# A decoder block in one kernel: the decays' scan in one piece, TensorE's order written out in the SSD scan

## The chip, the cores and the metric

The kernel runs on one core of a Trainium2 chip. The metric is the time of one execution on the device, in microseconds (us); the median of three runs is compared. TensorE (PE in the profile) multiplies matrices and accumulates in PSUM banks of 128x512; VectorE (DVE), ScalarE (ACT) and GpSimd (POOL) work element by element on tiles of 128 partitions in SBUF; SyncE (SP) issues the DMA transfers between DRAM and SBUF. Each engine works through its own list of instructions in order and waits on semaphores for the others.

## The reference, cut to what matters

The reference is one block of a hybrid model for 1024 tokens of width 1024: a Mamba-2 branch (SSD) and a gated linear attention branch (GLA), merged by gates, then attention to a memory, and a feed-forward part. The change touches the two recurrences:

```python
proj = n @ w_in
z, xBC, dt_raw, q, k, v, r, a1, g_ssd, g_gla = jnp.split(proj, idx, axis=-1)

# SSD, in chunks
xBC = silu(causal_dwconv(xBC, conv_w, conv_b))
a_cs = jnp.cumsum(dt * A, axis=-1)
CB = einsum('bclgn,bcsgn->bcgls', Cc, Bc)
y_diag = einsum('bcgls,bgrcls,bcsgrp->bclgrp', CB, segsum_exp(a), X)
states = einsum('bclgn,bgrcl,bclgrp->bcgrpn', Bc, decay_states, X)
prev = scan over chunks: state * chunk_decay + states
y_off = einsum('bclgn,bcgrpn,bgrcl->bclgrp', Cc, prev, exp(a_cs))
y = rmsnorm((y_diag + y_off + D * x) * silu(z), norm_g)

# GLA, the decays
log_alpha = log_sigmoid(a1 @ w_a2 + b_a) / 16
bcum = jnp.cumsum(log_alpha in chunks, axis=2)
```

All is float32. The kernel uses chunks of 128 tokens.

## The kernel before

**Products.** `proj` is computed in units of 256 output columns. A unit (class `Unit`) is a 2x2 block product done with seven products instead of eight; for a unit by itself they come in the order B11, T2, T1, B21, T3, B22, T4. A product is 12 matmuls of 128x512: four slices of the contraction, times three, since each float32 operand is split into a high and a low part (`h`, `l`) and the low-low part is left out. ScalarE makes the high part of the weights (`whi`), VectorE the low one (`wlo`), both after a 1 MB load `raw`; sums of weights (`sa`, and `raw` in place) are made by GpSimd or VectorE. ScalarE (B11, B21) and VectorE (the other five, `o<-acc,o`) take the results out of PSUM.

**Side work among the products.** `run(main, (side, rate))` takes `main` product by product and lets a generator `side` go on by `rate` of its yields after each. The stages that matter, by first unit: four units `zu` with the preparation of both recurrences as side work (`ssd_prep`, `gla_prep`); six units `xu`, each with the convolution of the unit ahead (`conv`: on VectorE, three passes for each of two blocks); then `ru` (4), `qk` (4) and `gs[:1]` with the SSD steps; `gs[1:]` and `gg[:3]` with the GLA steps; `gg[3]`; then the dense stages, whose first operands are `hl` and `wd`.

**SSD.** Each of the 16 steps (8 chunks by 2 groups of heads) has `load`, `lay` (transposes into banks; `cbm`, `bt`, `xd`), `decay` (eight ScalarE passes per step that make `e`, two exponentials, two VectorE products), `scan` (16 + 16 + 4 small matmuls into two banks, and the state), `gate` (`y`, on VectorE, then GpSimd), `stat` (a matmul with `ones`, then `rs` on VectorE and GpSimd) and `norm` (a matmul that spreads `rs`, `y<-y,bank`, store). In its turn, step i scans, the step before has its statistics, the next one is laid, step i is gated, the step before is normed, and the next one's decay is made, with yields between.

**Order.** A scheduler of the framework orders each engine's list from priorities; side work has a higher priority (`prio=PRIO`), and so have weights' splits and evacuations (`ahead()`, by 200). `pinned` keeps an instruction at its place in the program's order. The loads are all issued by SP's queue.

## Time and profile before

| | |
|---|---|
| three runs, median | 1956.74 us (1956.26 to 1957.37) |
| the profiled execution, its own time | 1956.3 us |
| its span in the trace | 1954.5 us |
| granted TensorE clock, mean | 0.996 |
| busy TensorE, VectorE, ScalarE, GpSimd | 98%, 67%, 43%, 29% |

In the trace the unit `xu[0]` begins at 249.6 us, `ru[0]` at 365.9, `ru[1]` at 385.4, `gs[0]` at 591.0, `gs[2]` at 634.1 and `gg[3]` at 789.3. An engine's share of busy time is an average over stages with different limits. The chain of waits follows the work that ended last backwards from the end; a row "acc<-T3h,wlo" is a matmul into bank `acc` with stationary operand T3 (high part) and moving operand `wlo`, or the other way round, as the names are given in the trace; a number in brackets at a row's end is the idle time ahead of it and what ended it.

### The profile page before, as it was taken

The page shows a single profiled execution, that of the slowest core. Times are in us where ns is not written, and L with a number is a line of the kernel's source. Part 1 is how long each engine was busy: PE and PEld are TensorE (multiplying, and loading weights), DVE is VectorE, ACT ScalarE, POOL GpSimd, SP SyncE. Part 2 cuts the span into 40 slices and gives each one's busy share as a digit, 9 for nine tenths or more (in the row PEclk, how much of TensorE's full clock was granted, in tenths as well). Part 3 has the DMA queues.
Part 4 walks back from the last instruction along what each step waited for, and adds up shares of the span by engine and source line. Part 5 has one row for each costly group of instructions (what it writes and reads, how often), then busy time and mean ns, then how long its engine had stood idle before and what let it go on. Part 6 is the DMA issues. An engine that isn't in the chain of part 4 may idle for free.

```text
span 1954.5 us, 26271 instructions
## 1 busy us (share of the span) xinstructions
PE 1919.9 (98%) x9772; PEld 1617.3 (83%) x9772; DVE 1317.2 (67%) x1868; ACT 848.4 (43%) x1493; POOL 574.1 (29%) x429
## 2 busy tenths in 40 slices
PE   8899999999999999999999999999999999999998
PEld 7898788778788888888888888888888888888887
DVE  6866779879886655565545237577777777766565
ACT  8434564465552543643224226454333333344243
POOL 1012334355553212112433000006445544320002
PEclk9999999999999999999999999999999999999999
DMA  9333372366553653897684201442233224177463
GB/s 316 139 121 101 119 290 98 133 196 198 169 168 114 209 162 119 328 371 252 242 298 150 78 24 44 140 141 81 87 125 112 82 100 143 42 270 243 159 222 119
DMA packets 238242, 317.97 MB, mean 163 GB/s; under 512 B 16906, under 2 KB 156404, under 8 KB 238116
## 3 DMA queue, kind: packets, MB, share of 16 engines
q1 hardware_dynamic: 238116, 316.31, 47.8%
q8 instruction: 77, 1.26, 0.3%
q14 instruction: 49, 0.40, 0.1%
HBM read 215.27 MB, written 100.99 MB: 162 GB/s over the span
## 4 chain that ended last, share of the span: by engine, by line
PE 83%; DVE 8%; DMA 3%; issue 2%; ACT 2%; POOL 2%; SPq 1%; POOLq 0%; DVEq 0%; ACTq 0%
PE acc L51 72%; PE bank L51 9%; DVE wlo L73 2%; DVE cv L73 1%; PE bank L55 1%; DVE o L73 1%; DMA xt<-in_x_dram 1%; DMA csb<-cs_d 1%; DVE hs L73 1%; DMA raw<-in_w_in_dram 1%; POOL sa L73 0%; ACT e L911 0%; POOL y L73 0%; POOL ssum L73 0%; DVE y L73 0%
## 5 line engine op out<-in xcount | busy, mean ns | idle before, releaser
L51 PE MATMUL acc<-hl,wd 128*128 128x512 f32 x1920 | 438.7, 390 | 0.0
L51 PEld LDWEIGHTS acc<-hl,wd 128*128 128x128 f32 x1920 | 360.4, 188 | 74.1
L73 DVE TENSOR_TENSOR wlo<-raw,whi 128x512 fp32r<-128x512 f32 x272 | 241.6, 894 | 80.7 <-ACT whi L221 78.7
L221 ACT ACTIVATE whi<-raw 128x512 fp32r<-128x512 f32 x272 | 169.5, 628 | 245.1 <-PE acc L51 214.3
L73 DVE TENSOR_TENSOR o<-acc,o 128x512 f32<-128x512 f32 (+1 forms) x256 | 172.8, 676 | 119.8 <-PE acc L51 108.2
L51 PE MATMUL acc<-fs 128*128 128x512 f32 (+1 forms) x792 | 155.7, 356 | 0.1
L51 PEld LDWEIGHTS acc<-fs 128*128 128x128 f32 x792 | 130.8, 189 | 20.7 <-issue 0.5
L73 POOL TENSOR_TENSOR raw<-raw,sa 128x512 f32<-128x512 f32 x44 | 58.7, 1334 | 228.6 <-DVE wlo L73 228.6
L73 DVE TENSOR_TENSOR fs<-fr,fs 128x1024 fp32r<-128x1024 f32 (+1 forms) x84 | 99.0, 1219 | 36.6 <-ACT fs L221 36.5
L221 ACT ACTIVATE fs<-fr 128x1024 fp32r<-128x1024 f32 (+1 forms) x84 | 78.8, 982 | 96.3 <-PE acc L51 32.1
L221 ACT ACTIVATE whi<-sa 128x512 fp32r<-128x512 f32 x96 | 60.0, 626 | 108.3 <-PE acc L51 102.7
L73 POOL TENSOR_TENSOR sa<-raw 128x512 f32<-128x512 f32 x43 | 67.8, 1577 | 105.0 <-DMA raw<-in_w_in_dram 78.0
L73 DVE TENSOR_TENSOR wlo<-sa,whi 128x512 fp32r<-128x512 f32 x96 | 82.2, 857 | 15.2 <-ACT whi L221 15.1
L73 DVE TENSOR_TENSOR wd<-raw,wd 128x1024 fp32r<-128x1024 f32 x40 | 53.1, 1329 | 50.9 <-ACT wd L221 50.8
L73 POOL TENSOR_TENSOR rstd<-rstd,mhalf 128x4 f32<-128x4 f32 (+1 forms) x7 | 8.7, 1246 | 251.2 <-DVE rstd L73 251.2
L221 ACT ACTIVATE wd<-raw 128x1024 fp32r<-128x1024 f32 x40 | 42.3, 1059 | 88.5 <-PE acc L51 82.7
L51 PE MATMUL acc<-B22h,wlo 128*128 128x512 f32 x192 | 76.6, 399 | 3.0 <-DVE wlo L73 3.0
L51 PE MATMUL acc<-T3h,wlo 128*128 128x512 f32 x192 | 76.0, 396 | 1.2 <-DVE wlo L73 1.2
L73 POOL TENSOR_TENSOR raw<-raw 128x512 f32<-128x512 f32 x44 | 75.9, 1725 | 2.8 <-DVE sa L73 2.8
L51 PE MATMUL acc<-T4h,whi 128*128 128x512 f32 x192 | 76.1, 396 | 0.4 <-DVE o L73 0.4
L51 PE MATMUL acc<-B22h,whi 128*128 128x512 f32 x192 | 76.1, 396 | 0.0
L51 PE MATMUL acc<-B11h,whi 128*128 128x512 f32 x192 | 75.8, 395 | 0.0
(389 smaller groups left out, 4735.4 us busy)
## 6 DMA issues: line engine op xcount, KB each, us to landing
raw<-in_w_in_dram SPq DMA_DIRECT2D x26, 1024.0 KB, 5.7
raw<-in_w_ffn_in_dram SPq DMA_DIRECT2D x22, 1024.0 KB, 8.1
act_d<-o SPq DMA_DIRECT2D x77, 256.0 KB, 2.2
fr<-act_d SPq DMA_DIRECT2D x35, 512.0 KB, 5.8
pre<-in_w_ffn_out_dram SPq DMA_DIRECT2D x11, 1024.0 KB
fr<-down_d SPq DMA_DIRECT2D x20, 512.0 KB, 4.7
down_d<-pre SPq DMA_DIRECT2D x33, 256.0 KB, 3.6
raw<-in_w_xkv_dram SPq DMA_DIRECT2D x8, 1024.0 KB, 8.1
```

The costliest lines, as they stand in the source:

```text
L51: return s.e.matmul(o, x, y, **kw)
L55: return s.e.transpose(o, x, i)
L73: return f(*a, **kw)
L221: ACT.activation(hi, src, AF.Copy)
```

## The change

- **The decays.** In `gla_prep` a head's cumulative sum is one scan over 1024 tokens instead of two over 512. The preparation so has four yields fewer, and its rate is 1.0 instead of 33/28.
- **Convolutions.** The units of B and C (4 and 5) come first. The pool with the states and the tiles `xz` and `bc` is opened ahead of the convolutions; the first step's loads are put behind the third and the fifth unit, its `csb` in an `xz` buffer. `bc` has three buffers and one DMA instead of two.
- **SSD steps.** Loads are issued two steps ahead; `csb` has a call of its own, behind the scan that frees its buffer. `cbm` stays in a part of its PSUM bank. Scan, the sum for the step before (`sum`) and the norm of the step two before stand together, then the next step's lay and this one's gate, then the statistics, the next decay and the state's update, then the square. There are six yields ahead of the first scan, and three instead of one in the first step.
- **Order.** During the SSD stage TensorE's list is in the program's order (`manual_schedule`).
- **Units.** The SSD steps have `gs[:2]` instead of `gs[:1]`, at a rate of 79/70 instead of 64/63; the GLA steps run over `gs[2:]` and `gg[:3]`, at 40/30 instead of 40/36.

```diff
--- before.py
+++ after.py
@@ -824,9 +824,8 @@
             yield
             pinned(DVE.scalar_tensor_tensor(x, x, 0.0, y, ALU.min, ALU.subtract))
             yield
-            for j in range(2):
-                pinned(DVE.tensor_tensor_scan(y[:, half(j)], keep[:, half(j)], x[:, half(j)], 0.0, ALU.mult, ALU.add))
-                yield
+            pinned(DVE.tensor_tensor_scan(y, keep, x, 0.0, ALU.mult, ALU.add))
+            yield
             yv, xv = (v.rearrange("p (c s) -> p c s", s=CH) for v in (y, x))
             bm, bl = yv[:, :, CH // 2 - 1:CH // 2], yv[:, :, CH - 1:CH]
             pinned(sub(DVE, xv, yv, bm.to_broadcast([P, NCH, CH])))
@@ -839,31 +838,22 @@
             ACT.activation(e, e, AF.Exp, scale=1.0 / TAU)
         yield
 
-    xu = [Unit(w_in, 0, XBC0 + 256 * u) for u in range(6)]
+    XU = (4, 5, 0, 1, 2, 3)
+    xu = [Unit(w_in, 0, XBC0 + 256 * u) for u in XU]
     zu = w_in_units(Z0, 4, store_rows(sz_d))
     ru = w_in_units(R0, 4, store_rows(sr_d))
     qk = w_in_units(Q0, 2, store_rows(q_d)) + w_in_units(K0, 2, store_rows(k_d))
     gs = w_in_units(GS0, 4, store_rows(gs_d))
     gg = w_in_units(GG0, 4, store_rows(gg_d))
     prep = chain([ssd_prep(), gla_prep()])
-    run(singles(zu, B, xu[:1]), (prep, 33 / 28))
+    run(singles(zu, B, xu[:1]), (prep, 1.0))
     drain(prep)
     settle_all()
     st2.close()
     st2 = ExitStack()
-    cvp = pool("conv", 1, stack=st2)
-    pend = iter(())
-    for u in range(6):
-        run(group([xu[u]], B, (xu + ru)[u + 1:u + 2]), (pend, 1.0))
-        drain(pend)
-        pend = conv(u, xu[u])
-    drain(pend)
-    st2.close()
-
-
     st3 = ExitStack()
-    sp_ = pool("ssd", 1, stack=st3)
-    state = [sp_.tile([P, GH, 64], F32, name=f"state{g}", tag=f"state{g}") for g in range(2)]
+    sl_ = pool("ssdl", 1, stack=st3)
+    state = [sl_.tile([P, GH, 64], F32, name=f"state{g}", tag=f"state{g}") for g in range(2)]
     for g in range(2):
         POOL.memset(state[g], 0.0)
 
@@ -880,23 +870,24 @@
 
         def load(s):
             g, tk = s.g, s.tk
-            s.L = sp_.tile([P, 8, CH], F32, name="xz", tag="xz", bufs=3)
+            s.L = sl_.tile([P, 8, CH], F32, name="xz", tag="xz", bufs=3)
             SP.dma_start(s.L[:, 0:4], xbc_d[g * 512:(g + 1) * 512, tk].rearrange("(k p) s -> p k s", p=P))
-            s.BC = sp_.tile([P, 2, CH], F32, name="bc", tag="bc", bufs=2)
-            for i in range(2):
-                r0 = 1024 + i * 256 + g * P
-                SP.dma_start(s.BC[:, i], xbc_d[r0:r0 + P, tk])
+            s.BC = sl_.tile([P, 2, CH], F32, name="bc", tag="bc", bufs=3)
+            SP.dma_start(s.BC, xbc_d[1024:1536, tk].rearrange("(i g p) s -> g p i s", g=2, p=P)[g])
+            SP.dma_start(s.L[:, 4:8], sz_d[g * 512:(g + 1) * 512, tk].rearrange("(k p) s -> p k s", p=P))
+
+        def load_cs(s):
             s.csb = sp_.tile([P, GH, CH], F32, name="csb", tag="csb", bufs=2)
+            s.fetch_cs()
+
+        def fetch_cs(s):
             SP.dma_start(s.csb.rearrange("p h s -> p (h s)"),
                          cs_d[s.i0:s.i0 + GH, :].rearrange("h s -> (h s)").partition_broadcast(P))
-            SP.dma_start(s.L[:, 4:8], sz_d[g * 512:(g + 1) * 512, tk].rearrange("(k p) s -> p k s", p=P))
 
         def lay(s):
-            p = bank()
+            p = s.p = bank()
             PE.matmul(p[:, :P], s.BC[:, 0], s.BC[:, 1], start=True, stop=True)
             PE.transpose(p[:, P:2 * P], s.BC[:, 0], ident)
-            s.cbm = sp_.tile([P, CH], F32, name="cbm", tag="cbm", bufs=2)
-            mul(DVE, s.cbm, p[:, :P], triu)
             s.bt = sp_.tile([P, P], F32, name="bt", tag="bt", bufs=2)
             ACT.activation(s.bt, p[:, P:2 * P], AF.Copy)
             p = bank()
@@ -914,7 +905,9 @@
             s.xc = sp_.tile([P, GH, 64], F32, name="xc", tag="xc", bufs=1)
             mul(POOL, s.xc, s.xd, s.heads(dec, 64))
             mul(DVE, s.csb, s.csb, s.BC[:, 1].unsqueeze(1).to_broadcast([P, GH, CH]))
-            mul(DVE, s.e, s.e, s.cbm.unsqueeze(1).to_broadcast([P, GH, CH]))
+            cbm = s.p[:, 2 * P:3 * P]
+            mul(DVE, cbm, s.p[:, :P], triu)
+            mul(DVE, s.e, s.e, cbm.unsqueeze(1).to_broadcast([P, GH, CH]))
 
         def scan(s):
             st = state[s.g]
@@ -930,7 +923,11 @@
                 PE.matmul(p[:, a * 256:(a + 1) * 256], s.bt, s.xc[:, 4 * a:4 * a + 4].rearrange("p h d -> p (h d)"),
                           start=True, stop=True)
             mul(POOL, st, st, s.heads(ec, 64))
-            add(DVE, st, p.rearrange("p (h d) -> p h d", d=64), st)
+            s.pst = p
+
+        def update(s):
+            st = state[s.g]
+            pinned(add(DVE, st, s.pst.rearrange("p (h d) -> p h d", d=64), st))
 
         def gate(s):
             s.y = sp_.tile([P, 4, CH], F32, name="y", tag="y", bufs=3)
@@ -938,10 +935,15 @@
                 DVE.scalar_tensor_tensor(s.y[:, k], s.L[:, k], dcol[:, s.g * 4 + k:s.g * 4 + k + 1],
                                          s.py[:, k * P:(k + 1) * P], ALU.mult, ALU.add)
             mul(POOL, s.y, s.y, s.L[:, 4:8])
-            sq = sp_.tile([P, 4, CH], F32, name="sq", tag="sq", bufs=1)
-            ACT.activation(sq, s.y, AF.Square)
+
+        def square(s):
+            s.sq = sp_.tile([P, 4, CH], F32, name="sq", tag="sq", bufs=1)
+            pinned(ACT.activation(s.sq, s.y, AF.Square))
+
+        def sum(s):
+            sq = s.sq
             s.rd = sp_.tile([P, CH], F32, name="rd", tag="rd", bufs=2)
-            add(DVE, sq[:, 0:2], sq[:, 0:2], sq[:, 2:4])
+            pinned(add(DVE, sq[:, 0:2], sq[:, 0:2], sq[:, 2:4]))
             add(DVE, s.rd, sq[:, 0], sq[:, 1])
 
         def stat(s):
@@ -957,38 +959,64 @@
             SP.dma_start(ys_d[s.g * 512:(s.g + 1) * 512, s.tk].rearrange("(k p) s -> p k s", p=P), s.y)
 
     def ssd_steps():
-        it = [SSD(c, g) for c in range(NCH) for g in range(2)]
-        it[0].load()
-        yield
+        n = len(it)
+        it[1].load()
+        it[1].load_cs()
+        for _ in range(1):
+            yield
         it[0].lay()
         yield
         it[0].decay()
-        yield
-        for i in range(len(it) + 1):
-            z = it[i - 1] if i else None
-            a = it[i] if i < len(it) else None
-            b = it[i + 1] if i + 1 < len(it) else None
-            if b:
-                b.load()
+        for _ in range(6):
+            yield
+        for i in range(n + 2):
+            y, z, a, b, c = (it[k] if 0 <= k < n else None for k in range(i - 2, i + 3))
             if a:
                 a.scan()
+            if z:
+                z.sum()
+            if y:
+                y.norm()
+            yield
+            if c:
+                c.load()
+            if b:
+                b.lay()
+            if a:
+                a.gate()
             yield
             if z:
                 z.stat()
             if b:
-                b.lay()
-            yield
+                b.decay()
+            if c:
+                c.load_cs()
             if a:
-                a.gate()
-            yield
-            if z:
-                z.norm()
-            if b:
-                b.decay()
-            yield
-
+                a.update()
+            for _ in range(3 if i == 0 else 1):
+                yield
+            if a:
+                a.square()
+                yield
+
+    it = [SSD(c, g) for c in range(NCH) for g in range(2)]
+    cvp = pool("conv", 1, stack=st2)
+    pend = iter(())
+    for n, u in enumerate(XU):
+        run(group([xu[n]], B, (xu + ru)[n + 1:n + 2]), (pend, 1.0))
+        drain(pend)
+        pend = conv(u, xu[n])
+        if n == 2:
+            it[0].csb = sl_.tile([P, GH, CH], F32, name="xz", tag="xz", bufs=3)
+            it[0].fetch_cs()
+        if n == 4:
+            it[0].load()
+    drain(pend)
+    st2.close()
+    sp_ = pool("ssd", 1, stack=st3)
     ssd = ssd_steps()
-    run(singles(ru + qk + gs[:1], B, gs[1:2]), (ssd, 16 * 4 / 63), prio=PRIO)
+    with tc.manual_schedule(engines={mybir.EngineType.PE}):
+        run(singles(ru + qk + gs[:2], B, gs[2:3]), (ssd, 79 / 70), prio=PRIO)
     drain(ssd)
     st3.close()
 
@@ -1113,7 +1141,7 @@
             yield
 
     gla = gla_steps()
-    run(singles(gs[1:] + gg[:3], B, gg[3:]), (gla, 8 * 5 / 36), prio=PRIO)
+    run(singles(gs[2:] + gg[:3], B, gg[3:]), (gla, 8 * 5 / 30), prio=PRIO)
     drain(gla)
     st4.close()
     st_early.close()
```

First place: VectorE in the preparation, in the last but one of the `zu` units, before (names: `gx`, `gy` are the decays of a head, a scan stands as SCALAR_TENSOR_TENSOR from `keep`, `wlo` are the low parts of weights, `o` the unit's output; of the unit `raw_2333` here, the low parts are those of B21, T3 and B22).

```order
L73 SCALAR_TENSOR_TENSOR gy0_2101<-keep_2058,gx0_2097 128x512 x2
L73 TENSOR_TENSOR gx0_2097<-gy0_2101 128x1024
L73 TENSOR_TENSOR wlo_2405<-raw_2333,whi_2404 128x512
L73 TENSOR_TENSOR o_2341<-acc_2369,o_2341 128x512
L73 SCALAR_TENSOR_TENSOR gx1_2098<-gx1_2098,gy1_2102 128x1024
L73 TENSOR_TENSOR wlo_2429<-raw_2333,whi_2428 128x512
L73 TENSOR_TENSOR o_2341<-acc_2388,o_2341 128x512
L73 SCALAR_TENSOR_TENSOR gy1_2102<-keep_2058,gx1_2098 128x512 x2
L73 TENSOR_TENSOR wlo_2449<-raw_2333,whi_2448 128x512
```

And with the change (the same unit is `raw_2331`, the low parts are those of B21, T3, B22 and T4):

```order
L73 SCALAR_TENSOR_TENSOR gy0_2101<-keep_2058,gx0_2097 128x1024
L73 TENSOR_TENSOR gx0_2097<-gy0_2101 128x1024
L73 TENSOR_TENSOR wlo_2402<-raw_2331,whi_2401 128x512
L73 TENSOR_TENSOR o_2335<-acc_2367,o_2335 128x512
L73 TENSOR_TENSOR wlo_2422<-raw_2331,whi_2421 128x512
L73 TENSOR_TENSOR o_2335<-acc_2386,o_2335 128x512
L73 SCALAR_TENSOR_TENSOR gx1_2098<-gx1_2098,gy1_2102 128x1024
L73 TENSOR_TENSOR wlo_2446<-raw_2331,whi_2445 128x512
L73 SCALAR_TENSOR_TENSOR gy1_2102<-keep_2058,gx1_2098 128x1024
L73 TENSOR_TENSOR wlo_2465<-raw_2331,whi_2464 128x512
```

T3's low part has moved from behind head 1's `gx` to ahead of it, and B22's from behind head 1's scan to ahead of it; the scan is one row.

Second place: TensorE in the SSD stage, before, where a step's `xz` transposes (lay) and the spread of `rs` (norm) stand (`bank` are PSUM banks of the SSD step, `acc` those of the units).

```order
L51 MATMUL acc_4103<-T4h_1355,wlo_4301 128x512
L51 MATMUL acc_4103<-T4h_1355,whi_4300 128x512
L51 MATMUL acc_4103<-T4l_1356,whi_4300 128x512
L55 MATMUL bank_4177<-ident_107,xz_4117 128x128 [waits DMAHW5_49,DVE_49,PE_49]
L55 MATMUL bank_4177<-ident_107,xz_4117 128x128 x3
L51 MATMUL acc_4103<-T4h_1355,wlo_4301 128x512
L51 MATMUL acc_4344<-B11h_436,whi_4340 128x512 [waits Activation_49]
L51 MATMUL acc_4344<-B11l_437,whi_4340 128x512
L51 MATMUL acc_4344<-B11h_436,wlo_4341 128x512
L51 MATMUL bank_4232<-ident_107,rs_4167 128x128 [waits Pool_49]
```

With the change, in unit `q0`, the end of a scan and what follows it:

```order
L51 MATMUL bank_4647<-csb_4449,state0_2642 64x128 x2
L51 MATMUL bank_4664<-xc_4601,bt_4548 128x256 [waits Activation_49,Pool_49]
L51 MATMUL bank_4664<-xc_4601,bt_4548 128x256
L51 MATMUL bank_4671<-ident_107,rs_4587 128x128 [waits Pool_49]
L51 MATMUL bank_4680<-bc_4542 128x128 [waits DMAHW6_49,DVE_49]
L55 MATMUL bank_4680<-ident_107,bc_4542 128x128
L55 MATMUL bank_4685<-ident_107,xz_4540 128x128 [waits DMAHW1_49,DVE_49,PE_49]
L55 MATMUL bank_4685<-ident_107,xz_4540 128x128 x3
L51 MATMUL acc_4571<-T3h_1258,whi_4699 128x512 [waits Activation_49]
L51 MATMUL acc_4571<-T3l_1259,whi_4699 128x512
```

Before, matmuls of products stood between lay and norm; now scan, norm and the next lay follow one another here, and the next product comes behind them.

Third place: VectorE at the end of `gg[3]` and the begin of the first dense stage, before (`hl` and `wd` are its operands, `acc_7544` and `acc_7518` banks of the unit).

```order
L73 TENSOR_TENSOR o_7481<-acc_7544,o_7481 128x512 [waits PE_49]
L73 TENSOR_TENSOR wlo_7616<-raw_7469,whi_7615 128x512 [waits Activation_49]
L73 TENSOR_TENSOR wd_7611<-raw_7500,wd_7611 128x1024 [waits DMAHW2_49,Activation_49]
L73 TENSOR_TENSOR wd_7664<-raw_7500,wd_7664 128x1024 [waits DMAHW6_49,Activation_49]
L73 TENSOR_TENSOR wlo_7634<-raw_7469,whi_7633 128x512 [waits PE_49,Activation_49]
L73 TENSOR_TENSOR o_7481<-acc_7518,o_7481 128x512 [waits DVE_49,PE_49]
L73 SCALAR_TENSOR_TENSOR hl_7506<-hl_7506,cols_118 128x1024 [waits DMAHW3_49,Activation_49]
L73 TENSOR_TENSOR o_7481<-acc_7544,o_7481 128x512 [waits PE_49]
L73 SCALAR_TENSOR_TENSOR hl_7532<-hl_7532,cols_118 128x1024 [waits DMAHW6_49,Activation_49]
```

And with the change (`o_7452` with `acc_7489` in its last row here is the evacuation of T4):

```order
L73 TENSOR_TENSOR o_7452<-acc_7515,o_7452 128x512 [waits PE_49]
L73 SCALAR_TENSOR_TENSOR hl_7529<-hl_7529,cols_118 128x1024 [waits DMAHW1_49,Activation_49]
L73 TENSOR_TENSOR o_7452<-acc_7489,o_7452 128x512 [waits PE_49]
L73 SCALAR_TENSOR_TENSOR hl_7533<-hl_7533,cols_118 128x1024 [waits DMAHW2_49,Activation_49]
L73 TENSOR_TENSOR wd_7582<-raw_7471,wd_7582 128x1024 [waits DMAHW4_49,Activation_49]
L73 TENSOR_TENSOR wd_7635<-raw_7471,wd_7635 128x1024 [waits DMAHW3_49,Activation_49]
```

The first low parts of `wd` stood ahead of the unit's last low part; now they stand behind its last evacuation and one more `hl`.

## The prediction

> **What bounds the kernel now.** I read the page first: the busy table (engine, busy us, share, count) and the chain of work that ended last.
>
> ```profile
> span 1954.5 us, 26271 instructions
> PE 1919.9 (98%) x9772; PEld 1617.3 (83%) x9772; DVE 1317.2 (67%) x1868; ACT 848.4 (43%) x1493; POOL 574.1 (29%) x429
> PE 83%; DVE 8%; DMA 3%; issue 2%; ACT 2%; POOL 2%; SPq 1%; POOLq 0%; DVEq 0%; ACTq 0%
> ```
>
> TensorE is the bound: whatever helps must shorten TensorE's own work or its waits. The change touches no product, so its matmul work stays. All that is to be won or lost are the times in which TensorE stands, in the stages that the change touches. So next I read the view by windows, cut at the stages (columns: window, length, busy us of PE, PEld, DVE, ACT, POOL, then granted clock, DMA share, GB/s).
>
> ```profile
> 208.00:227.00 19.00, 15.90 (x68) 12.26 (x67) 16.37 (x15) 10.19 (x14) 10.19 (x9) 1.00 0.35 119
> 229.00:231.00 2.00, 2.00 (x6) 1.57 (x5) 1.30 (x3) 0.63 (x1) 0.00 (x0) 0.50 0.71 281
> 249.00:365.00 116.00, 115.19 (x505) 94.18 (x504) 100.77 (x105) 63.21 (x86) 44.27 (x27) 1.00 0.50 184
> 385.00:634.00 249.00, 245.15 (x1511) 200.02 (x1510) 197.08 (x318) 128.30 (x274) 127.01 (x101) 1.00 0.55 171
> 634.00:789.00 155.00, 155.00 (x773) 132.62 (x772) 90.93 (x188) 73.17 (x181) 36.46 (x28) 1.00 0.50 160
> ```
>
> Three places have something to win: the decay preparation (TensorE idles 3.1 of 19 us, and right behind it the granted clock is 0.50), the convolutions (0.8 of 116) and the SSD stage (3.85 of 249). GLA, 634 to 789, has nothing: 155.00 of 155.
>
> Busy time understates a stand, since a matmul's record (390 ns) outlasts the next one's start. The measure I use is the issue interval, from the chain by time:
>
> ```profile
> 788.04 42.18 PE acc L51 x186
> 557.42 2.97 PE bank L51 x38
> 569.64 2.97 PE bank L51 x38
> 582.05 2.97 PE bank L51 x38
> 557.42:569.64 12.22, 12.03 (x80) 9.67 (x81) 1.00 0.59 184
> ```
>
> A 128x512 matmul takes 42.18/186 = 0.227 us, a product of 12 takes 2.72, a unit of 84 takes 19.0. Undisturbed SSD steps start 12.22 and 12.41 us apart. Of the 80 matmuls in the first of these, 36 are products' (8.16 us), so a step itself costs TensorE 4.06 to 4.25.
>
> **The change part by part.** *Decay scans whole.* TensorE and VectorE in the preparation (start, duration):
>
> ```profile
> 220.04 0.39 PE L51 MATMUL acc<-T3l,whi 128*128 128x512 f32 x1
> 221.58 0.50 PE L51 MATMUL acc<-T3h,wlo 128*128 128x512 f32 x1 [1.16 <-DVE wlo L73]
> 224.22 0.39 PE L51 MATMUL acc<-B22l,whi 128*128 128x512 f32 x1
> 226.56 0.50 PE L51 MATMUL acc<-B22h,wlo 128*128 128x512 f32 x1 [1.95 <-DVE wlo L73]
> 229.04 0.63 PE L51 MATMUL acc<-B22l,whi 128*128 128x512 f32 x1
> 229.47 0.63 PE L51 MATMUL acc<-B22h,wlo 128*128 128x512 f32 x1
> ```
> ```profile
> 213.11 2.34 DVE L73 TENSOR_TENSOR_SCAN gy<-keep,gx 128x512 f32<-128x512 f32 x2
> 217.24 0.68 DVE L73 TENSOR_TENSOR o<-acc,o 128x512 f32<-128x512 f32 x1
> 217.84 2.00 DVE L73 SCALAR_TENSOR_TENSOR gx<-gx,gy 128x1024 f32<-128x1024 f32 x1
> 219.76 1.77 DVE L73 TENSOR_TENSOR wlo<-raw,whi 128x512 fp32r<-128x512 f32 x1
> 222.05 3.87 DVE L73 TENSOR_TENSOR_SCAN gy<-keep,gx 128x512 f32<-128x512 f32 x2
> 225.84 0.66 DVE L73 TENSOR_TENSOR wlo<-raw,whi 128x512 fp32r<-128x512 f32 x1
> ```
>
> T3's low part stands behind gx's 2.00, B22's behind two half scans of 3.87 together. TensorE's gaps are 1.54 and 2.34 us, less 0.23 each: 1.31 + 2.11 = 3.4. Then matmuls issue 0.43 apart instead of 0.23 for about 3 us, seven of them: 1.4 more. Together 4.8; the slow stretch stands right behind the two gaps, so I take it to go with them.
>
> One scan of 1024 elements is not in the trace; two halves took 2.34 to 3.87, so it takes about that, and the fusion alone saves at most one instruction's fixed cost. What matters is the order that it brings (first place of the order above): T3's low part now stands ahead of gx1 and B22's ahead of the scan. VectorE is then done with T3's at about 217.5, where TensorE wants it at 220.3; B22's, at worst 0.68 + 2.00 + 1.77 later, at 222, wanted at 223.0; T4's behind a scan of 2.34 to 3.87 at 225 to 226.5, wanted at 225.7. That leaves 0 to 0.8 us of a new stand, 0.3 taken. **Preparation: -4.5**, bounds -4.8 and 0 (slow forms again in front).
>
> The Trainium skill, "TensorE: Matmul & The Clock Gate", section "Part 1: The HAM clock gate", gives half clock after an idle window of about 3.4 us. No gap here is that long, yet the clock was 0.50 after gaps of 1.5 and 2.3: the trace is stricter than that table. By the Trainium skill these gaps would not be what slowed the clock, the 1.4 would stay and the kernel would take 1951.1.
>
> *Convolutions in another order.* They keep their VectorE passes (three taps by two blocks for each of six units) between the same products, and the loads put among them run on a queue whose weights are issued units ahead. Cost nothing, hidden behind products of 116 us; uncovered, one late weight load would cost up to its 5.7 us below.
>
> *SSD stage.* From ru1's first matmul (385.4) to gs2's (634.1) are 248.8 us. Nine units are 9 x 84 x 0.227 = 171.4; 16 steps of 4.25 are 68.0; 9.4 us are stands (12.4 with 4.06). Seen as waits (releaser: us, times, longest):
>
> ```profile
> PE bank L51 <- POOL rs L73: 2.2, 3, 0.9
> PE bank L51 <- DVE y L73: 1.2, 3, 0.5
> PEld bank L51 <- POOL rs L73: 4.2, 5, 1.3
> PEld bank L51 <- DVE y L73: 1.5, 3, 0.5
> 542.75 5.76 DMA raw<-in_w_in_dram
> ```
>
> They are the norm's broadcast, which needs rs from GpSimd while GpSimd waits for a weight load, and transposes that wait for a bank which the gate still reads. With square and statistics a yield further behind the gate, GpSimd has a product more for y, and from statistics to norm stand 24 matmuls and a scan, 8.4 us, at every step, where it was between 18 matmuls (4.1) and 42 (9.5). The old waits should mostly go: 9.4 is the upper gain.
>
> In the fixed order TensorE can no longer slide a product in front of a late operand. I walked the order with these durations:
>
> ```profile
> L73 DVE TENSOR_TENSOR e<-e,cbm 128x1024 f32<-128x1024 f32 x16 | 31.1, 1944 | 2.1 <-ACT e L912 1.6
> L73 DVE SCALAR_TENSOR_TENSOR y<-xz,dcol,bank 128x128 f32<-128x128 f32 x64 | 17.8, 337 | 0.8 <-PE bank L51 0.8
> L911 ACT ACTIVATE e<-csb,cs 128x128 f32<-128x128 f32 x128 | 39.3, 390 | 17.3 <-DMA csb<-cs_d 17.2
> csb<-cs_d SPq DMA_DIRECT2D x16, 512.0 KB, 4.6
> raw<-in_w_in_dram SPq DMA_DIRECT2D x9, 1024.0 KB, 5.7
> ```
>
> - The third and fifth scans stand two products (5.5 us) behind their lay, the others three (8.2). Their csb load is issued only when the scan two steps earlier is through, lands 4.6 later, eight passes take about 2.4, the splits queued on both engines and the e product about 3.5: 0.8 and 0.3 us late.
> - The norm of the third step waits for rs behind GpSimd's wait for a weight load: 0 to 1.6, 0.8 taken.
> - Twice (second place of the order) lay follows scan and norm with no product between, and its second bank waits for the gate's four y of 0.337 on VectorE, queued behind the rest: 1.5 each, 3.0.
> - Weights' high parts behind the eight passes on ScalarE: 0.5.
>
> New stands 5.4, old ones 9.4: **SSD stage -4.0**, bounds -9.4 (none is new) and +3 (each price doubled, 10.8, and rs still late, 1.6).
>
> The e product now reads cbm from a PSUM bank. Its row has mean 1944 against 1248 for the like-sized csb product and 0.68 for o with a PSUM operand while GpSimd worked, so I take 1.2: VectorE gets 16 x 0.7 = 11 us back, all in slack. The Trainium skill, "GPSIMD Engine Reference", section "Key points", has GpSimd's SBUF interfaces shared with VectorE instructions of two SBUF inputs, and o at 0.68 beside wlo at 1.77 agrees. If it were not so, the e product would stay at 1.9, the third scan would be 0.7 later, and the sum 1950.4.
>
> *GLA on other units.* The same bursts over six units instead of nine, in a stage with no stand; covered by products. *The first dense stage* (third place of the order): its first weights' low part is now split behind T4's last evacuation and an hl, where it stood well ahead of T4.
>
> ```profile
> 804.60 2.36 DVE L73 TENSOR_TENSOR wd<-raw,wd 128x1024 fp32r<-128x1024 f32 x2 [0.36 <-ACT wd L221]
> 808.29 1.98 PE L51 MATMUL acc<-hl,wd 128*128 128x512 f32 x8
> 808.08 1.28 DVE L73 SCALAR_TENSOR_TENSOR hl<-hl,cols 128x1024 fp32r<-128x1024 f32 x1
> ```
>
> VectorE needs 0.68 + 1.28 + 1.18 = 3.1 after T4; TensorE has eight matmuls, 1.8, without it: 1.3, **+1.5** with the wake-up, bounds 0 and 3.
>
> **Sum:** -4.5 - 4.0 + 1.5 = -7.0. The profiled execution took 1956.3 (span 1954.5 and 1.8 around it), 0.4 under the median of the runs. So 1949.3 for a like execution, 1949.7 as median: **1949.7**.
>
> **The rivals.**
> *All stands go.* Preparation -4.8, SSD -9.4, dense 0: 1942.5. For it speaks that the walk assumed every queue full; against it the lay that directly follows a norm.
> *The stands only move.* SSD's new ones equal the old: -4.5 + 1.5 = -3.0, 1953.7. For it: the stage's VectorE is busy 197 of 249 us and its chains are as long as before.
> *The fusion does not act as said.* If gx and scan take their slow forms (2.00, 3.87) in front of a low part again, preparation gains 0 and the sum is -2.5: 1954.2. Against it: the order of the rows.
> *The fixed order turns lateness into stands at every scan* (slower). Place: the e product and xc of each of 16 scans, with GpSimd held by weight loads (5.76 in the chain). It decides from a mean lateness of (9.4 + 4.5 - 1.5)/16 = 0.8 us a scan; at 1.5 us it is 24 - 12.4 = +11.6: 1968.3. For it: 17.2 us of ScalarE's waits for csb, hidden so far because other matmuls went ahead. Against it: three products of distance, 8.2 us. The stage's waits of up to 1.3 us left the clock at 1.00. The Trainium skill, "TensorE: Matmul & The Clock Gate", section "A second HAM failure mode: psum-queue depth-cycling", tells of short idles between groups of matmuls that slow the clock; it would add to this case, and no row of this stage shows it yet.
>
> **How the numbers follow.** Forecast 0.50, all stands go 0.12, only move 0.15, fusion idle 0.08, slower 0.15. A change under 0.2% (3.9 us) can't be told from none. The forecast lies 7.0 below, so nine tenths of it count as faster (0.45), with all of the second (0.12) and a third of the two small cases (0.08): faster 0.65; same 0.19, slower 0.16. Range: the low end is the second case, 1942.5; the high end goes halfway into the last, 1960, which leaves out about 0.12. Faster cases alone: 1942 to 1953.
>
> **What would show it.** Right: in the window of the preparation no wait for wlo above 1 us and a clock of 1.00; in the SSD stage the norm's waits for rs nearly gone, one or two waits of transposes for y; steps 13.75 us apart (half a unit and one step). The first dense stage starts with one wait for wd. Wrong: bank<-e,xd or bank<-xc waiting at most scans, above 0.8 us each; the clock below 1.00 in the SSD stage; weight loads late at SP's queue.

## The result, and the profile after

The change made the kernel a little slower: 1962.25 us median of 14 runs (1958.0 to 1969.3) against 1957.05 of 14 runs of the kernel before (1954.4 to 1958.8), ratio 1.003, 95% interval 1.0021 to 1.0039. The forecast was 1949.7, with a range of 1942.5 to 1960.0. The page of the profiled execution, its span and its busy table:

```profile
span 1959.2 us, 26254 instructions
PE 1917.5 (98%) x9772; PEld 1616.0 (82%) x9772; DVE 1304.0 (67%) x1864; ACT 848.5 (43%) x1493; POOL 568.6 (29%) x429
```

The span grew by 4.7 us and TensorE's busy time shrank by 2.4: the time went into stands. To see where, the view by windows is cut at the same instructions in both traces, the first matmul of `zu[2]`, of `xu[0]`, of `ru[0]`, of `gs[2]` and of the feed-forward part (window, length, busy us of the engines, granted clock, DMA share, GB/s). The kernel before:

```profile
208.66:249.62 40.96, 37.86 (x157) 30.22 (x156) 36.09 (x36) 16.84 (x24) 18.90 (x17) 0.96 0.37 129
249.62:365.85 116.23, 115.42 (x505) 94.37 (x504) 100.35 (x105) 63.21 (x86) 44.27 (x27) 1.00 0.50 184
365.85:634.14 268.29, 264.24 (x1594) 215.52 (x1593) 215.00 (x336) 138.11 (x287) 135.32 (x107) 1.00 0.53 167
634.14:1301.53 667.39, 666.98 (x3157) 560.83 (x3156) 364.32 (x579) 273.23 (x522) 125.71 (x89) 1.00 0.54 183
```

And the kernel with the change:

```profile
209.06:246.88 37.82, 36.17 (x157) 29.05 (x156) 35.67 (x32) 16.85 (x24) 18.83 (x17) 1.00 0.42 143
246.88:363.73 116.85, 115.59 (x505) 94.21 (x504) 99.75 (x105) 62.65 (x86) 43.38 (x29) 1.00 0.55 197
363.73:635.15 271.42, 262.00 (x1592) 216.37 (x1590) 208.02 (x334) 137.66 (x288) 129.35 (x101) 0.99 0.49 158
635.15:1306.17 671.02, 668.91 (x3161) 560.13 (x3160) 359.62 (x581) 274.65 (x522) 125.41 (x93) 1.00 0.53 183
```

The lengths differ by -3.1 (preparation), +0.6 (convolutions), +3.1 (SSD) and +3.6 us (behind `gs[2]`); with 0.4 ahead of the first window and 0.1 behind the last that is 4.7.

**Preparation.** The two stands of before are gone but for 0.35 us, and so is the slow stretch (clock 1.00 instead of 0.96; the run with the scan alone, below, tells how much of that belongs to the change). A new stand has come, on TensorE and VectorE by time (start, duration):

```profile
226.29 0.39 PE L51 MATMUL acc<-B11l,whi 128*128 128x512 f32 x1
228.13 0.50 PE L51 MATMUL acc<-T4h,whi 128*128 128x512 f32 x1 [1.46 <-DVE o L73]
```
```profile
223.52 3.37 DVE L73 TENSOR_TENSOR_SCAN gy<-keep,gx 128x1024 f32<-128x1024 f32 x1
226.82 0.66 DVE L73 TENSOR_TENSOR wlo<-raw,whi 128x512 fp32r<-128x512 f32 x1
227.40 0.68 DVE L73 TENSOR_TENSOR o<-acc,o 128x512 f32<-128x512 f32 x1
```

T4 waits for the bank that T3 filled; its evacuation `o` stands behind the whole scan, which took 3.37 us.

**SSD stage.** The waits of TensorE (releaser: us in all, times, longest), and then one of them by time, on TensorE, VectorE and GpSimd:

```profile
PE bank L55 <- issue: 4.8, 3, 1.9
PE bank L55 <- PE bank L55: 1.7, 3, 0.8
PE bank L51 <- DVE e L73: 0.9, 2, 0.8
```
```profile
516.44 0.39 PE L51 MATMUL bank<-bc 128*128 128x128 f32 x2
516.67 0.27 PE L55 MATMUL bank<-ident,bc 128*128 128x128 f32 x1
518.83 0.63 PE L55 MATMUL bank<-ident,xz 128*128 128x128 f32 x4 [1.89 <-issue]
519.21 0.48 PE L51 MATMUL acc<-T3h,whi 128*128 128x512 f32 x1
```
```profile
514.35 3.34 DVE L73 TENSOR_TENSOR wlo<-raw,whi 128x512 fp32r<-128x512 f32 x2
517.62 1.11 DVE L73 SCALAR_TENSOR_TENSOR y<-xz,dcol,bank 128x128 f32<-128x128 f32 x4
```
```profile
514.20 1.26 POOL L73 TENSOR_TENSOR sa<-sa,raw 128x512 f32<-128x512 f32 x1
515.43 1.71 POOL L73 TENSOR_TENSOR raw<-raw 128x512 f32<-128x512 f32 x1
```
```profile
519.00:523.00 4.00, 4.00 (x15) 3.17 (x14) 2.91 (x5) 2.87 (x9) 2.14 (x2) 0.64 0.65 181
```

Line 55 is the transposes. The profile puts their wait down to "issue" or to themselves, since it sees no semaphore event; the order names VectorE, and the four `y` of the gate end at 518.73, 0.1 us ahead of them. They are late because two low parts stand ahead of them, 1.67 us each while GpSimd makes weights' sums. Measured by issue interval, six steps have such a stand of the transposes (0.5 to 2.05 us, together 7.5); the first scan adds 1.5 for an operand of its state's matmuls, the product ahead of it 0.8, a late e product 0.8. Behind the longest, the granted clock was 0.64 of full speed in the mean of these 4 us (0.50 from 520.1 to 523.5): 1.5 us more.

**The first dense stage**, TensorE and ScalarE:

```profile
813.83 2.14 PE L51 MATMUL acc<-hl,wd 128*128 128x512 f32 x8 [0.92 <-ACT wd L221]
816.41 0.96 PE L51 MATMUL acc<-hl,wd 128*128 128x512 f32 x3 [0.43 <-DVE wd L73]
```
```profile
809.15 3.69 ACT L1246 ACTIVATE hl<-hl,cols 128x1024 fp32r<-128x1024 f32 x3 [0.39 <-DMA hl<-ys_d]
812.75 1.99 ACT L221 ACTIVATE wd<-raw 128x1024 fp32r<-128x1024 f32 x2
```

It waits for the high part of `wd` and then for the low one, 1.7 us in all by issue interval (1.08 and 0.61), since both stand behind `hl` passes. A further 0.4 comes at 1065 us, in a later dense stage.

### The profile page after: what moved, and what is told of

The parts are those of the page before. It is cut to its first block, busy times and chain, and to the rows that moved or that the text cites. A ratio compares the mean times of both kernels' runs of the same rounds, so it can differ in the third digit from the quotient of the medians.

```text
span 1959.2 us, 26254 instructions
## 1 busy us (share of the span) xinstructions
PE 1917.5 (98%) x9772; PEld 1616.0 (82%) x9772; DVE 1304.0 (67%) x1864; ACT 848.5 (43%) x1493; POOL 568.6 (29%) x429
## 4 chain that ended last, share of the span: by engine, by line
PE 44%; DMA 3%; POOL 2%; DVE 2%; issue 1%; ACT 1%; SPq 0%; POOLq 0%; ACTq 0%; DVEq 0%
PE acc L51 39%; PE bank L51 4%; POOL pre L73 1%; DMA pre<-in_w_ffn_out_dram 1%; DMA h_d<-ga 1%; DMA down_d<-pre 1%; POOL ssum L73 1%; PE bank L55 1%; DMA wlo<-gg_d 0%; POOL sa L73 0%; DVE hl L73 0%; DVE wd L73 0%; DMA ga<-ysg_d 0%; DVE gates L73 0%; DMA gates<-gg_d 0%
## 5 line engine op out<-in xcount | busy, mean ns | idle before, releaser
L73 DVE TENSOR_TENSOR wlo<-raw,whi 128x512 fp32r<-128x512 f32 x272 | 245.7, 910 | 86.8 <-ACT whi L221 86.7
L51 PE MATMUL acc<-T3h,whi 128*128 128x512 f32 x192 | 76.5, 399 | 0.0
L51 PE MATMUL acc<-T1h,whi 128*128 128x512 f32 x192 | 76.1, 396 | 0.0
L51 PE MATMUL acc<-T2h,whi 128*128 128x512 f32 x192 | 75.8, 395 | 0.0
```

What stands on the lines that cost most here:

```text
L51: return s.e.matmul(o, x, y, **kw)
L73: return f(*a, **kw)
```

## The experiments

Each kernel was timed over five rounds beside the kernel before; ratios are to that. "The stage" is from `ru[0]` to `gs[2]` (268.3 us before, 271.4 with the change), "behind" is from `gs[2]` to the feed-forward part (667.4 and 671.0).

### The fixed order taken away

```diff
-    with tc.manual_schedule(engines={mybir.EngineType.PE}):
-        run(singles(ru + qk + gs[:2], B, gs[2:3]), (ssd, 79 / 70), prio=PRIO)
+    run(singles(ru + qk + gs[:2], B, gs[2:3]), (ssd, 79 / 70), prio=PRIO)
```

> The changed kernel with TensorE's list left to the scheduler again (no fixed order in the SSD stage). Theory 1, the fixed order turns late operands into stands: from ru0 to gs2 the time falls from 271.4 us to 268.3 (as before the change) or less, no transposes of xz wait above 1 us, and the ratio to the kernel before is 1.000 or below. Theory 2, the steps' new composition costs the time in any order: 271 us or more, and the ratio stays at 1.003.

Theory 1 holds: ratio 0.9947 (0.9935 to 0.996), 1947.4 us. The stage took 259.2:

```profile
363.57:622.77 259.20, 258.74 (x1586) 214.30 (x1585) 204.31 (x335) 138.22 (x288) 124.95 (x105) 1.00 0.52 165
```

So the new steps gain 9.1 us and their fixed order takes 12.2 back. How the free order does it, on TensorE behind a scan:

```profile
500.40 0.39 PE L51 MATMUL bank<-bc 128*128 128x128 f32 x2
504.61 0.60 PE L55 MATMUL bank<-ident,xz 128*128 128x128 f32 x4
```

The transposes stand 4.2 us behind the matmuls that the program has beside them; `y` has long been done. Behind, the kernel lost 4.7 us to the one before (2.1 of waits for `wd` and a slow clock near 1030 us).

### The units' banks for the transposes

```diff
-            p = bank()
+            p = acc()
             for k in range(4):
                 PE.transpose(p[:, k * P:(k + 1) * P], s.L[:, k], ident)
```

> The changed kernel, fixed order kept, with the xz transposes of lay in one of the four banks of the units instead of the four of the SSD steps. Theory 1, lay waits because its bank is the one that the gate of the step just scanned still reads: the seven waits of lay (together some 8 us) and the clock's drop at 520 us go, ru0 to gs2 falls to about 262 us, the ratio to 0.998, and the runs spread less than 11 us. Theory 2, VectorE is simply too full in this stage and another operand is late next: the waits move to xd or to the low parts, and ru0 to gs2 stays above 269.

Ratio 1.0026 (1.0016 to 1.0035), the stage 270.4. The rival was right: the transposes no longer wait, the scan does, for e.

```profile
PE bank L51 <- DVE e L73: 3.8, 3, 2.4
```

### The whole scan alone

In the kernel before, only the two edits of the decays:

```diff
-            for j in range(2):
-                pinned(DVE.tensor_tensor_scan(y[:, half(j)], ...))
+            pinned(DVE.tensor_tensor_scan(y, keep, x, 0.0, ALU.mult, ALU.add))
...
-    run(singles(zu, B, xu[:1]), (prep, 33 / 28))
+    run(singles(zu, B, xu[:1]), (prep, 1.0))
```

> The kernel before with only the decays' scan whole (and the preparation's rate of 1.0 that goes with it). Expected by the traces: the two stands of 1.3 and 2.1 us and seven matmuls at half clock go, one of 1.6 us comes ahead of T4, the preparation gains 2.8 to 3.3 us and nothing else moves: ratio 0.9985. Rival: the gain is given back in the stages behind, because all that follows is ordered anew: ratio 1.000.

Ratio 0.9986 (0.9977 to 0.9995). The preparation went from 40.97 to 37.78 us, the convolutions from 116.2 to 117.0, the stage from 268.3 to 269.2, behind 667.4: a gain of 3.2 us in its window, part of which is given back. The gain in the whole time is small, but its interval excludes 1.

About half of the 3.2 is the slow clock of that one execution of the kernel before. The next two experiments keep the two half scans, and with them both stands (3.1 us of idle time, as before), but no slow clock followed, and the window took 39.36 us (fixed order alone) and 39.33 us (units alone) instead of 40.97. The 5 us from 225 on, in the kernel before and in the run with the fixed order alone:

```profile
225.00:230.00 5.00, 3.44 (x11) 2.75 (x12) 4.44 (x6) 0.24 (x1) 2.29 (x3) 0.79 0.31 122
225.00:230.00 5.00, 3.63 (x16) 3.01 (x17) 5.00 (x8) 0.63 (x1) 2.30 (x3) 1.00 0.34 136
```

Against these two, the edit gains about 1.5 us.

### The units alone

```diff
-    run(singles(ru + qk + gs[:1], B, gs[1:2]), (ssd, 16 * 4 / 63), prio=PRIO)
+    run(singles(ru + qk + gs[:2], B, gs[2:3]), (ssd, 16 * 4 / 70), prio=PRIO)
...
-    run(singles(gs[1:] + gg[:3], B, gg[3:]), (gla, 8 * 5 / 36), prio=PRIO)
+    run(singles(gs[2:] + gg[:3], B, gg[3:]), (gla, 8 * 5 / 30), prio=PRIO)
```

> The kernel before with only the units dealt out anew: the SSD steps over gs[:2] too, the GLA steps over six units. Theory: this alone makes the first dense stage wait for wd behind T4 (some 2 us from gg3 on) and leaves the SSD stage's stands as they are, ratio 1.001. Rival: the further distance between SSD steps (3.5 products more than 3) takes SSD stands away, ratio 0.999 or less.

Ratio 1.0068 (1.0055 to 1.0082): far worse than either expectation. The stage took 271.8, and behind 679.6, with one wait in the first dense stage and a slow clock after it:

```profile
PE acc L51 <- ACT wd L221: 6.9, 1, 6.9
```

### The fixed order alone

```diff
+    with tc.manual_schedule(engines={mybir.EngineType.PE}):
-    run(singles(ru + qk + gs[:1], B, gs[1:2]), (ssd, 16 * 4 / 63), prio=PRIO)
+        run(singles(ru + qk + gs[:1], B, gs[1:2]), (ssd, 16 * 4 / 63), prio=PRIO)
```

> The kernel before with only TensorE's fixed order in the SSD stage. Theory 1, the fixed order by itself costs some 12 us in this stage, whatever the steps are: ru0 to gs2 goes from 268 to 278 us or more, ratio 1.005 or more. Theory 2, it costs only with the new steps, whose lay stands right behind the scan: ru0 to gs2 within 3 us of 268, ratio 0.999 to 1.002.

Ratio 1.0047 (1.0035 to 1.0059), the stage 276.4. But neither theory had the place: most of it is a single wait, ahead of the first step, for loads that need the last convolutions:

```profile
PE bank L51 <- DMA bc<-xbc_d: 13.3, 1, 13.3
```
```profile
400.00:590.00 190.00, 190.00 (x1180) 158.36 (x1179) 146.99 (x253) 101.69 (x221) 98.75 (x78) 1.00 0.54 174
```

Behind the first steps TensorE is busy 190.00 of 190 us. The old steps lose nothing in fixed order; they lose their old stands. Their distance is another, too: the fixed order puts their scans 15.2 us, four products, apart, where the free order of the kernel before had them 12.0 to 14.8 us apart in these 190 us. (The run also shows what the earlier loads of the change are for.)

### Parts of the new steps undone, in free order

Three kernels, each the one with the fixed order taken away and one more edit. The units as before:

```diff
-    run(singles(ru + qk + gs[:2], B, gs[2:3]), (ssd, 79 / 70), prio=PRIO)
+    run(singles(ru + qk + gs[:1], B, gs[1:2]), (ssd, 79 / 63), prio=PRIO)
...
-    run(singles(gs[2:] + gg[:3], B, gg[3:]), (gla, 8 * 5 / 30), prio=PRIO)
+    run(singles(gs[1:] + gg[:3], B, gg[3:]), (gla, 8 * 5 / 36), prio=PRIO)
```

> The changed kernel with free order, and the units dealt out as before the change: SSD over nine and a half units at 79/63, GLA over 36 products at 40/36. Theory: the loss behind gs2 (672.1 us from gs2 to the feed-forward part against 667.4 before) comes from GLA's later end, so it returns to 667.5 to 668 and the waits for wd go; the SSD stage keeps its gain; ratio 0.992 to 0.993. Rival: with steps closer together the SSD stage gives back 3 us or more: ratio 0.995 or above.

Ratio 0.9948 (0.9936 to 0.996): the stage 263.7, behind 663.4 without a wait for `wd`, the sum 4.2 us less than with the new units in that one execution, the ratio the same. The waits for `wd` went, as the theory had it, and the stage gave back 4.5 us, as the rival had it (a first part of GLA now lies ahead of `gs[2]`). Then `cbm` in an SBUF tile made in lay:

```diff
+            s.cbm = sp_.tile([P, CH], F32, name="cbm", tag="cbm", bufs=2)
+            mul(DVE, s.cbm, p[:, :P], triu)
             s.bt = sp_.tile([P, P], F32, name="bt", tag="bt", bufs=2)
...
-            cbm = s.p[:, 2 * P:3 * P]
-            mul(DVE, cbm, s.p[:, :P], triu)
-            mul(DVE, s.e, s.e, cbm.unsqueeze(1).to_broadcast([P, GH, CH]))
+            mul(DVE, s.e, s.e, s.cbm.unsqueeze(1).to_broadcast([P, GH, CH]))
```

> The changed kernel with free order, and cbm in SBUF again, made in lay. Theory A, the recomposed steps gain in the SSD stage because the e product falls from 1.9 to 1.2 us and VectorE is no longer late: without it ru0 to gs2 rises from 259.2 to 264 or more, ratio 0.997. Theory B, the gain comes from the distance of norm and lay in the steps: ru0 to gs2 stays below 261, ratio 0.995.

Ratio 0.9957 (0.9944 to 0.997, one run of 10760 us aside), the stage 260.2: cbm's place is worth some 1 us, though the e product is faster by what was forecast. In the changed kernel:

```profile
L73 DVE TENSOR_TENSOR e<-e,bank 128x1024 f32<-128x1024 f32 x16 | 19.4, 1211 | 1.7 <-ACT e L903 1.6
```

Then the norm one step behind, at the place of the square:

```diff
-            if y:
-                y.norm()
             yield
...
+            if z:
+                z.norm()
             if a:
                 a.square()
```

> The changed kernel with free order, and the norm one step behind the scan again instead of two, at the place of the square. Theory B, the waits for rs come back (6 us in all before the change): ru0 to gs2 rises from 259.2 to 263 or more, ratio 0.9965. Theory A, the norm's place is of no weight once the steps lie 3.5 products apart: below 261, ratio 0.995.

Ratio 0.9942 (0.9931 to 0.9954), 1944.2 us, the stage 258.5: the norm's distance gains nothing. This is the fastest version found, as far as the intervals tell no different from the free order alone. This one with the units as before:

> The changed kernel in free order, with the norm one step behind and the units dealt out as before the change: the two best variants together. Expected, if the loss of the first dense stage comes from the units: from gs2 to the feed-forward part as in the run with those units alone, the SSD stage as with the norm one step behind, ratio 0.993 to 0.994. Rival: the waits for rs come back where steps lie closer (3.1 products), ratio 0.996.

Ratio 0.9957 (0.9944 to 0.9969), the stage 265.0, behind 667.4. Not better: two waits for `y`, 3.0 us, and a slow clock at 480 us.

### The sequence of a step

The old sequence in the changed kernel, fixed order kept, at one yield a product (the lines that it replaces are left out; four yields instead of six stand ahead of the first scan):

```diff
...
+            if a:
+                a.scan()
+            if c:
+                c.load()
+            yield
+            if z:
+                z.sum()
+                z.stat()
+            if b:
+                b.lay()
+            yield
+            if a:
+                a.gate()
+                a.update()
+            yield
+            if z:
+                z.norm()
+            if b:
+                b.decay()
+            if c:
+                c.load_cs()
+            if a:
+                a.square()
+            yield
...
+        run(singles(ru + qk + gs[:2], B, gs[2:3]), (ssd, 1.0), prio=PRIO)
```

> The changed kernel, fixed order kept, units, loads and cbm as changed, but within a step the sequence of before: scan, then statistics and lay, then gate, then norm and decay, one product between each. Theory S, the fixed order is harmless where a product stands between scan and lay (as the run of the kernel before in fixed order showed behind its first load) and costs only with the changed sequence: ru0 to gs2 falls from 271.4 to 263 or less, ratio 0.998 or less. Theory F, fixed order goes badly with anything else of the change (loads, cbm in PSUM, 3.5 products a step): 269 or more, ratio 1.001 or more.

Ratio 1.0196 (1.0182 to 1.021), the stage 295.3. The transposes no longer waited, but I had put the sum right ahead of the statistics that read it:

```profile
PE bank L51 <- DVE rd L73: 19.2, 9, 3.9
```

And the changed sequence with lay one yield later:

```diff
             if c:
                 c.load()
-            if b:
-                b.lay()
             if a:
                 a.gate()
             yield
             if z:
                 z.stat()
+            if b:
+                b.lay()
```

> The changed kernel, fixed order kept, with lay one yield later, beside the statistics, so that a product stands between scan and lay, and one less between lay and the next scan. Theory S': only the place of lay behind the scan counts: its waits (8 us) go, ru0 to gs2 about 263. Theory D: what counts is that VectorE's chain from scan over gate, lay and the e product to the next scan fills the step; then the wait moves to the scan's e and xc, 1 to 2 us at most steps, and ru0 to gs2 is 275 or more.

Ratio 1.0174 (1.0159 to 1.0189), the stage 306.9. Theory D was right, and stronger than expected:

```profile
PE bank L51 <- DVE e L73: 35.5, 11, 7.2
```

With the sum of the old sequence moved up beside the scan:

```diff
             if a:
                 a.scan()
+            if z:
+                z.sum()
...
             if z:
-                z.sum()
                 z.stat()
```

> The earlier run with the old sequence of a step, mended in one place: the sum for the step before stands beside the scan, one product ahead of the statistics' matmul, which waited for it in nine steps (19.2 us). Theory S, the old sequence has no other late operand in fixed order: these waits go, ru0 to gs2 falls from 295 to 265 or less, ratio 1.004 or less (what it loses behind gs2 stays). Theory F: another operand takes their place, 275 or more.

Ratio 1.005 (1.0037 to 1.0064); the stage 266.5 with all its waits at the first scan (by issue interval nothing above 0.3 us behind 398 us), so the sequence is free of late operands at this distance. Behind, 680.5: 7.0 us for `wd` and a slow clock.

One product forced between each scan and the lay behind it:

```diff
-                        next(g, None)
+                        if next(g, None) == "scan":
+                            break
...
                 y.norm()
-            yield
+            yield "scan"
```

> The changed kernel, fixed order kept, with one product always between a scan (with the norm behind it) and the lay that follows: where the rate gave two yields at once there, the second waits for the next product. Nothing else is edited. Theory S, the lay that follows the scan directly is a large part of the fixed order's price: the two stands of 1.9 and 2.1 us go, with the clock's drop behind them (1.5), ru0 to gs2 falls from 271.4 to 267 or less and the spread of the runs from 11 us to 6. Theory D, VectorE's gate passes come too late in any case: stands of lay remain at 5 us or more in sum, ru0 to gs2 stays above 269.

Ratio 1.0044 (1.0032 to 1.0056), the stage 274.8. Theory D: lay's stands are still 6.4 us together, and e adds 3.8. (The runs spread over 3.5 us, which theory S had expected.) Only the transposes one yield later:

```diff
             if z:
                 z.stat()
             if b:
+                b.turn()
                 b.decay()
```

(`turn` is the second half of `lay`.)

> The changed kernel, fixed order kept, with lay split: its B and C matmuls stay behind the scan, its four xz transposes stand one yield later, beside the statistics, where the free order had put them (4 us behind the B and C matmuls). Theory E, it is the xz transposes' early place in the list that costs, not the fixed order: lay's stands (7.5 us) and the clock's drop go, no wait for e above 1 us takes their place, ru0 to gs2 falls from 271.4 to 264 or less, ratio 0.999 or less unless the first dense stage waits longer. Rival: xd and xc then come late for the next scan: 269 or more.

Ratio 1.0054 (1.004 to 1.0067), the stage 275.1. The rival again; the waits of the stage, by releaser:

```profile
PE bank L51 <- POOL xc L73: 6.5, 5, 2.1
PE bank L51 <- DVE xd L73: 3.1, 2, 2.1
PE bank L51 <- DVE e L73: 2.0, 3, 1.5
```

### The weights' sums on VectorE

```diff
+    for u in ru + qk + gs[:2]:
+        u.e = DVE
     with tc.manual_schedule(engines={mybir.EngineType.PE}):
```

> The changed kernel, fixed order kept, with the weights' sums of the SSD stage's ten units on VectorE instead of GpSimd. Theory C, the gate's passes are late because the low parts ahead of them take 1.7 us instead of 0.7 beside GpSimd's sums: the low parts fall from a mean of 1.05 to 0.8 us or less, lay's stands from 7.5 to 3 us or less, ru0 to gs2 to 267 or less. Rival: VectorE gets some 28 us more work (four sums of 0.7 in ten units) and is later still: ru0 to gs2 273 or more.

Ratio 1.0016 (1.0006 to 1.0027), the stage 266.7, behind 678.2. The low parts fell from a mean of 1046 ns to

```profile
L73 DVE TENSOR_TENSOR wlo<-raw,whi 128x512 fp32r<-128x512 f32 x50 | 37.3, 750 | 19.7 <-ACT whi L221 19.7
```

and lay's stands from 7.5 to 5.4 us. Theory C had the direction, not the size: GpSimd's sums are a part of the lateness, about 2 of the 7.5.

### The distance between steps

Whatever was moved, waits stayed or came elsewhere, and the two kernels in fixed order that had none behind the first scan (the old steps alone, the mended old sequence) ran at four products a step instead of 3.54. So the two were exchanged. The changed kernel:

```diff
-        run(singles(ru + qk + gs[:2], B, gs[2:3]), (ssd, 79 / 70), prio=PRIO)
+        run(singles(ru + qk + gs[:2], B, gs[2:3]), (ssd, 1.0), prio=PRIO)
```

> The changed kernel, changed sequence and fixed order kept, with the SSD steps at one yield a product: four products from step to step instead of 3.54 (the last ten yields stand behind gs1, the last scan falls behind gs2's first products). Theory P, the steps are too close for the chain from scan over gate, bank, transposes, xd and xc to the next scan; the fixed order only shows it: at four products the waits for lay, e and xc behind the second scan fall from 10 us in sum to 2 or less, and the clock keeps 1.00. Theory Q, the changed sequence itself is late wherever it stands: 6 us or more remain.

And the mended old sequence:

```diff
-        run(singles(ru + qk + gs[:2], B, gs[2:3]), (ssd, 1.0), prio=PRIO)
+        run(singles(ru + qk + gs[:2], B, gs[2:3]), (ssd, 79 / 70), prio=PRIO)
```

> The mended run of the old sequence in fixed order, with the rate of the change: 3.54 products from step to step instead of four. Theory P: the stands come back, 6 us or more in sum behind the second scan (none before). Theory Q: the old sequence stays without them, 2 us or less.

TensorE over 190 us of the stage, of the changed kernel at four products and then of the old sequence at 3.54:

```profile
400.00:590.00 190.00, 190.00 (x1176) 158.19 (x1175) 143.31 (x244) 97.34 (x212) 99.51 (x80) 1.00 0.54 172
```
```profile
400.00:590.00 190.00, 183.09 (x1157) 150.75 (x1154) 141.89 (x240) 93.58 (x205) 92.83 (x78) 0.99 0.53 166
```

At four products the changed sequence has no wait at all behind the first scan (scans 15.15 us apart: 4 x 2.72 + 4.26); the old one at 3.54 has some 11 us of stands behind it, its stage takes 279.7 us instead of 266.5, and the clock falls. In fixed order the distance decides, as theory P had it, in both directions. The first kernel still comes out at 0.9993 (0.9984 to 1.0002), since behind the stage (which ends one scan earlier there) it took 683.2 us, with 5.9 us in one wait for `wd`; the second at 1.0046 (1.0033 to 1.0059).

Theory P's other half, that the chain itself needs more than 3.54 products and the fixed order only shows it, does not hold. The changed kernel with the fixed order taken away, over the same 190 us:

```profile
400.00:590.00 190.00, 189.74 (x1228) 157.64 (x1227) 152.52 (x265) 101.94 (x221) 95.19 (x82) 1.00 0.55 174
```

Its scans begin 13.95 us apart in the mean there (4.26 + 3.56 x 2.72), and ten of the thirteen distances are 12.0 to 12.9 us, about three products; TensorE idles 0.26 us in all. So the chain can be run in three products. One such step, from scan to scan on TensorE, and its gate on VectorE:

```profile
497.31 0.44 PE L51 MATMUL bank<-e,xd 128*64 128x128 f32 x4
504.61 0.60 PE L55 MATMUL bank<-ident,xz 128*128 128x128 f32 x4
510.18 0.44 PE L51 MATMUL bank<-e,xd 128*64 128x128 f32 x4
```
```profile
499.33 1.12 DVE L73 SCALAR_TENSOR_TENSOR y<-xz,dcol,bank 128x128 f32<-128x128 f32 x4 [0.56 <-PE bank L51]
```

One difference is visible at the gate: in the mean of all steps but the first, `y` begins 0.6 us (at most 1.7) behind the end of the scan's matmuls that fill its bank, against 1.8 us (at most 4.4) in the changed kernel and 1.0 us (at most 2.8) in fixed order at four products. Why VectorE comes to the gate so much later when TensorE's order is fixed was not taken apart, and no free order at four products was run.

## Why the prediction was wrong

- **Preparation, -4.5: right about the stands, lucky with the clock, too large.** The two stands went, as said (3.4 less 0.35), and the scan's 3.37 lies in the stated 2.34 to 3.87. The 1.4 of slow clock I took to go with the stands. It did go, but it was no fixed price of theirs: the same stands left the clock at 1.00 in two runs that keep the half scans. The remaining term, "0 to 0.8 us of a new stand, 0.3 taken", measured 1.6. I had followed T4's low part and not T3's evacuation, which stands one place further behind the same scan and holds T4's bank. Alone, the edit gained 3.2 in its window against the slowed execution and about 1.5 against the other two.
- **Convolutions, 0:** +0.6 in this execution, 0.8 in the one with the scan alone, which has the old convolution order; so it is not that order's doing.
- **SSD stage, -4.0: the step that failed.** It measured +3.1. Its first half was right: the old stands, put at 9.4, were what free order won (9.1). The failing step is "New stands 5.4". They measured about 12: 7.5 for the transposes (I had 3.0, at two places), 2.3 around the first scan (0), 0.8 for e (1.1, at other scans), 0 for rs (0.8), 1.5 of slow clock (0), and small ones. I had priced the transposes as an accident of two places without a product behind the scan. The runs show otherwise: a product there left 6.4 us of them, and each attempt to move the transposes made e, xd or xc late. What had no stands was either the fixed order at four products, in both sequences, or the free order at 3.54. So the price belongs to the two together: in fixed order VectorE comes later to its part of a step (the gate 1.8 us behind the scan instead of 0.6), and at 3.54 products TensorE stands for what hangs on it. It is not one chain alone: with the transposes in another bank the scan waited for e. Why VectorE is later in fixed order stays open.
- **"With square and statistics a yield further behind the gate ... the old waits should mostly go":** they went (rs still releases one weight load of this stage, 0.2 us), and with the norm put back in free order they stayed away too. The distance of the norm was not the cause; which of the remaining parts (loads two ahead, csb's own call, the first steps apart, the pitch in free order) won the 9.1 was not taken apart.
- **cbm in PSUM:** 1211 ns against the 1.2 us taken, and nearly all in slack, as said: worth about 1 us of the stage in free order.
- **First dense stage, +1.5:** 1.7 at the place named, 0.4 further on, of 3.6 behind `gs[2]`; the last step's norm, which now falls behind `gs[2]`'s first matmul, accounts for some 0.3 by its matmuls' intervals, and about 1 us has no single row. The term was an accident of one order, not a price: in the kernels run here this part took between 663 and 683 us (in some a scan or a part of GLA falls on the other side of the cut), with waits for `wd` of up to 7 us. Dealing out the units anew can do it alone, but the same units with the norm one step behind had none. What puts `wd` late in an order was not settled.
- **The slower rival was the right one in kind, at half its size and with the wrong place.** It had the fixed order turning lateness into stands and decided from 0.8 us a scan on. The fixed order cost 12.2 us over 16 scans, 0.76 each; with a preparation 1.4 and a rear 2.1 worse than forecast, that is on the slower side. Its sign, waits for e or xc at most scans, did not show in the changed kernel (one wait for e; the rest were the transposes'); e and xc became late as soon as the transposes were not. It had GpSimd's weight loads as the cause, where GpSimd's sums had a part and the distance of the steps decided.

## What to carry to other kernels

Before an engine's order is fixed, look at how late the other engines come to their part of a step, queued work included, and compare that with the distance that the rate gives the steps; here the free order ran without stands at a distance at which the fixed one stood in about every second step. If moving one instruction only changes the name of what is waited for, try a greater distance, or a free order, before another place. A stretch of slow clock behind a stand is no sure gain: see first whether other executions with the same stand have it. And an edit that has the scheduler draw its order anew should be read stage by stage, since the far stages move by as much as the edited one.
